# A hybrid decoder block on one core: weight sums of the first four up steps made by accumulating transfers

## The chip, the core and the metric

The kernel runs on one core of a Trainium2 chip. Its time is the device time of one execution in microseconds (us), and a kernel is compared by the median of its runs. The engines of the core are TensorE (PE; PEld is its weight load), VectorE (DVE), ScalarE (ACT), GpSimd (POOL) and SyncE (SP, which here only issues transfers).

## What is computed

One decoder block, in float32, for 1024 tokens of width 1024: attention heads and a chunked gating side by side, their output projection, and then a gated MLP with a causal convolution of three taps, with a norm ahead of each part. Cut to what matters here:

```python
D_MODEL = 1024; SEQ = 1024; D_FF = 2816; CONV_WIDTH = 3

def conv_ffn(x, w_up, conv_w, conv_b, w_down):
    h = x @ w_up                                   # [1024, 1024] @ [1024, 5632]
    h = depthwise_causal_conv(h, conv_w) + conv_b  # 3 taps along the tokens
    a, g = jnp.split(h, 2, axis=-1)
    return (jax.nn.silu(g) * a) @ w_down

    mix = jnp.concatenate([att, sg], axis=-1)      # attention, chunked gating
    h = h + mix @ w_out[layer]
    h = h + conv_ffn(rmsnorm(h, norm_ffn_g[layer]), w_up[layer], ...)
    return rmsnorm(h, norm_final_g)
```

The change concerns `x @ w_up`.

## The kernel before

**Numbers and products.** Every float32 operand of a matmul is split into two parts of a shorter format: ScalarE copies the value to the high part (L153) and VectorE subtracts that from the value to get the low part (L159), both in `split_w`. A product then takes three matmuls: high by high, high by low, low by high.

**The up projection by seven products.** It is made in 22 steps (`NFF`), each for 128 columns of `a` and 128 of `g`. A step takes a weight block of four parts, A11, A12, A21 and A22, and multiplies by the scheme of Strassen and Winograd: seven products instead of eight, three of which take a part as it is (A11, A12, A22) and four of which take a sum of parts:

S1 = A21 + A22, S2 = S1 + A11, S3 = A21 + A11, S4 = S2 + A12.

Each part of a step is a tile of 128 x 512 (256 KB). On the other side stand the activations (XB): B11, B21, B22 and T1 to T4, which are sums of token blocks. In `product` (L999) one product is twelve matmuls. The line is that of all products of the up stage; the names of their outputs tell them apart: `qa` for A11 and A12, `qb` (in step 0 `qc`) for S2, `qc` for S3 and A22, `qd` for S1 and S4.

**Loads and sums of a step.** `upw_a(i)` (L861) loads A11 and A12 as one tile of the ring `raw` (four buffers of 128 x 2 x 512) and later splits them into the ring `wha` (four buffers). `upw_b(i)` (L877) loads A21 and A22 into another `raw` tile and has GpSimd make the four sums (L881 to L889): three or four of them into the ring `sg` (four buffers of 128 x 512), and in step 1 three of them in the place of parts that are no longer needed. `split` of `upw_b` splits A22 and the sums into the ring `whb` (six buffers). In the memory of a step the blocks 0, 1, 2 and 3 of `wup` are A21, A22, A11 and A12.

**Order.** Each engine has its own queue and does its instructions in order. The order of an engine's queue is set by a scheduler from the source order, buffers and dependences, with a few edges added by hand (`behind`, `gates`), so that it isn't that of the source. The order of the products on TensorE is set by hand; the loads and sums of a step are set in motion by a generator, `nxt_of(i)`, which does the preparation of step i + 1 in pieces between the products of step i. The first two steps (`AHEAD = 2`) are prepared earlier: their loads and sums are issued before the tokens' loop below, and their products with A11 and A12 are made ahead of the others and kept in PSUM (`waited`).

**The tokens' loop, ahead of the up steps.** From about 405 to 460 us the output projection is finished for eight tiles of 128 tokens (order 0, 4, 1, 5, 2, 3, 6, 7): matmuls, the residual (`hadd`), the norm (`norm2`), and `flip`, which transposes a tile and makes the activation sums: for the tiles 4 to 7, T2 = B22 + B11 goes into `t2`, a tile with one buffer (VectorE, L958), and GpSimd subtracts from it (L961) to get `xtB21`, the unsplit T4. After the last flip come the splits of S2, S3 and S1 of step 0, those of T1, T4 and B22 (L1023, in two halves each), and then the steps.

**A step** (`up_b(i)`): the products S2, S3, S1, A22 and S4, with the subtractions u2 (L1061), u3 (L1065) and the others on VectorE between them, the convolutions `cg` and `ca` (the last multiplication of a step is L1087), and A11 and A12 of the next step in between (`up_a`). After the last step the down projection follows (L1189), from about 860 us.

Of the kernel before, what the change touches and what calls it, by code (L numbers as in the profile page):

```python
# [12 lines left out]
ALU = mybir.AluOpType  # L13
# [51 lines left out]
def block_kernel(ctx: ExitStack, tc: tile.TileContext, xT, xtok, wuv, wv, wqk, wf, cpk, bfv,  # L65
                 ggain, g2r, gfr, wsp, woa, wos, wup, wdn, out):
    nc = tc.nc
    act, dve, pool, pe, sp = Line(nc.scalar, tc), Line(nc.vector, tc), Line(nc.gpsimd, tc), nc.tensor, nc.sync
# [22 lines left out]
    def sb(tag, shape, dt=F32):  # L91
        return (raws if tag == "raw" else late if tag in LATE else early).tile(shape, dt, tag=tag, bufs=BUFS[tag], name=nm(tag))
# [57 lines left out]
    def split_w(src, hl, hi_eng="act", lo_eng="dve"):  # L150
        h, l = hl
        if hi_eng == "act":
            act.copy(h, src)  # L153
        elif hi_eng == "pool":
            pool.tensor_copy(h, src)
        else:
            dve.tensor_copy(h, src)
        eng = dve if lo_eng == "dve" else pool
        return eng.tensor_tensor(out=l, in0=src, in1=f32(h), op=ALU.subtract)  # L159
# [3 lines left out]
    def behind(inst, key):  # L163

        if key in gates:
            after(tc, inst, gates[key])
# [30 lines left out]
    def ring(dt=F32R):  # L197
        rn[0] += 1
        return sb(RTAG[(rn[0] - 1) % 6], [P, 2, 512], dt)
# [32 lines left out]
    for p_ in range(2):  # L232
        t = sb("G", [P, 2, 2, 512])
# [199 lines left out]
    W = [Weights(0)]  # L433
# [177 lines left out]
    for k in range(4):  # L611
        t = sb("raw", [P, 2, 512])
# [29 lines left out]
    for p_ in range(2):  # L642
        t = ring(F32)
# [207 lines left out]
    def ut_(pool_, tag, shape, dt, bufs):  # L851
        return pool_.tile(shape, dt, tag=tag, bufs=bufs, name=nm(tag))
# [3 lines left out]
    AHEAD = 2  # L856
# [13 lines left out]

        return out, split

    def upw_b(i, out, inplace=False):

        a11, a12 = out["ra"][:, 0, :], out["ra"][:, 1, :]
        wr = sb("raw", [P, 2, 512])
        sp.dma_start(out=wr, in_=wup[i, :, 0:2, :])  # L877
        a21, a22 = wr[:, 0, :], wr[:, 1, :]
        if inplace:
            s = [a21, ut_(upl, "sg", [P, 512], F32, 4), a11, a12]  # L880
            pool.tensor_tensor(out=a11, in0=a21, in1=a11, op=ALU.add)  # L881
            pool.tensor_tensor(out=s[1], in0=a11, in1=a22, op=ALU.add)
            pool.tensor_tensor(out=a21, in0=a21, in1=a22, op=ALU.add)
        else:
            s = [ut_(upl, "sg", [P, 512], F32, 4) for _ in range(4)]
            pool.tensor_tensor(out=s[0], in0=a21, in1=a22, op=ALU.add)  # L886
            pool.tensor_tensor(out=s[1], in0=s[0], in1=a11, op=ALU.add)  # L887
            pool.tensor_tensor(out=s[2], in0=a21, in1=a11, op=ALU.add)
        pool.tensor_tensor(out=s[3], in0=s[1], in1=a12, op=ALU.add)  # L889
        src = {"A22": a22, "S1": s[0], "S2": s[1], "S3": s[2], "S4": s[3]}  # L890

        def split(names):
            for n in names:
                t = ut_(upr, "whb", [P, 2, 512], F32R, 6)
                behind(split_w(src[n], (t[:, 0], t[:, 1])), "sums")
                out[n] = t
            return out

        return split
# [36 lines left out]
    def flip(tt):  # L936

        c = slice((tt % 4) * P, (tt % 4) * P + P)
        pp = []
        for kh in range(2):  # L940
            ps = sbank()
            for j in range(4):
                k = 4 * kh + j
                pe.transpose(ps[:, j * P:(j + 1) * P], xn[tt][:, k * P:(k + 1) * P], ident)
            pp.append(ps.rearrange("p (k t) -> p k t", k=4))
        if tt < 4:
            for n, p3 in (("B11", pp[0]), ("B21", pp[1])):
                hl_of(n, c, p3)
            for n, p3 in (("B11", pp[0]), ("B21", pp[1])):
                act.copy(xt[n][:, :, c], p3)  # L950
            return
        b11, b21, b22 = (xt[n][:, :, c] for n in ("B11", "B21", "B22"))
        t3 = ut_(xtp, "t3", [P, 4, P], F32, 1)
        t2 = ut_(xtp, "t2", [P, 4, P], F32, 1)
        act.copy(b22, pp[1])
        dve.tensor_tensor(out=b11, in0=b11, in1=pp[0], op=ALU.subtract)
        dve.tensor_tensor(out=t3, in0=b22, in1=pp[0], op=ALU.subtract)
        d = dve.tensor_tensor(out=t2, in0=b22, in1=b11, op=ALU.add)  # L958
        hl_of("T2", c, t2)
        hl_of("T3", c, t3)  # L960
        pool.tensor_tensor(out=b21, in0=t2, in1=b21, op=ALU.subtract)  # L961
        return d

    WA = [upw_a(i) for i in range(AHEAD)]
    W = [WA[0][1](("A11", "A12"))]
    first = (0, 4, 1, 5)
    banks8 = {(tt, hf): (bank() if hf == 0 else sbank()) for tt in first for hf in range(2)}
    for tt in first:
        for hf in range(2):
            wmm(tt, hf, banks8[tt, hf], (0, 1, 2))  # L970
    W.append(WA[1][1](("A11", "A12")))
    WB = [upw_b(0, W[0]), upw_b(1, W[1], True)]
    prev = None
    for tt in (0, 4, 1, 5, 2, 3, 6, 7):
        hload(tt)
# [32 lines left out]
    for i in range(AHEAD):  # L1008
# [4 lines left out]
        if i == 0:  # L1013

            last = flip(7)
            WB[0](("S2", "S3"))
            gates["sums"] = last

    def late_sum(n, src):
        for j in range(2):  # L1020
            k = slice(2 * j, 2 * j + 2)
            act.copy(XB[n][:, 0, k, :], xt[src][:, k, :])
            dve.tensor_tensor(out=XB[n][:, 1, k, :], in0=xt[src][:, k, :], in1=f32(XB[n][:, 0, k, :]), op=ALU.subtract)  # L1023

    late_sum("T1", "B11")
    WB[0](("S1",))
    late_sum("T4", "B21")
# [81 lines left out]
    def waited(i):  # L1109

        x1 = ut_(pst_[0], "u", [P, 512], F32, 5)
        ha = ut_(pst_[0], "h", [P, 1024], F32, 3)
        act.copy(x1, ahead[2 * i])
        dve.tensor_tensor(out=ha[:, 0:512], in0=ahead[2 * i + 1], in1=x1, op=ALU.add)
        return None, x1, ha

    st = waited(0)
    WB[0](("A22", "S4"))

    def nxt_of(i):  # L1120

        if i + 1 == NFF:
            while True:
                yield None
        if i + 1 < AHEAD:
            w, wb = W[i + 1], WB[i + 1]
            wa = lambda names: None
        else:
            w, wa = upw_a(i + 1)
            wb = upw_b(i + 1, w)  # L1130
            W.append(w)
        yield None
        wa(("A11",))
        wb(("S2",))
        yield waited(i + 1) if i + 1 < AHEAD else up_a(i + 1, w)
        wa(("A12",))
        wb(("S3",))
        yield None
        wb(("S1", "A22", "S4"))
        yield None  # L1140
# [21 lines left out]
    for p_, n in ((upl, "B11"), (upl, "T2"), (upl, "B21"), (upl, "T3"), (upr, "T1"), (upr, "T4"), (upr, "B22")):  # L1162
        t = ut_(p_, "x" + n, [P, 2, 4, 512], F32, 1)
# [37 lines left out]
    def blk(b):  # L1201
        return lambda p_: wd[p_][:, b, :]
# [129 lines left out]
```

## Time and profile before

| | |
|---|---|
| median of three runs | 1097.8 us (1097.66 to 1100.26) |
| the profiled execution: own time | 1102.1 us |
| the profiled execution: span of its instructions | 1100.4 us |
| mean granted TensorE clock, of full speed | 0.992 |
| bytes read and written in HBM | 114.95 MB and 42.27 MB, 143 GB/s over the span |

The profile is that of one execution. Its busy times are of each engine's instructions by themselves; a row of a group tells the line, the engine, what is written and read, how many there are, their busy time and mean, and then the engine's idle time just before them with what ended most of it. A row of the timeline has the start and the duration of one instruction or of a run of like ones, and in brackets the idle time before it. A row of the table by stretches has the length of the stretch and then the busy time of TensorE, of its weight load, of VectorE, ScalarE and GpSimd, each with the number of instructions in brackets, then the granted clock, the busy share of the 16 transfer engines and the GB/s that they moved. In a row of transfers stand the size of one and the median time from issue to landing. GpSimd issues no transfer of its own in this kernel: the queue of SP carries nearly all of them.

### The profile page before, as it was taken

The page shows a single profiled execution, that of the slowest core. Times are in us where ns is not written, and L with a number is a line of the kernel's source. Part 1 is how long each engine was busy: PE and PEld are TensorE (multiplying, and loading weights), DVE is VectorE, ACT ScalarE, POOL GpSimd, SP SyncE. Part 2 cuts the span into 40 slices and gives each one's busy share as a digit, 9 for nine tenths or more (in the row PEclk, how much of TensorE's full clock was granted, in tenths as well). Part 3 has the DMA queues.
Part 4 walks back from the last instruction along what each step waited for, and adds up shares of the span by engine and source line. Part 5 has one row for each costly group of instructions (what it writes and reads, how often), then busy time and mean ns, then how long its engine had stood idle before and what let it go on. Part 6 is the DMA issues. An engine that isn't in the chain of part 4 may idle for free.

```text
span 1100.4 us, 14437 instructions
## 1 busy us (share of the span) xinstructions
PE 1070.2 (97%) x5013; PEld 880.7 (80%) x5013; DVE 897.8 (82%) x1355; ACT 572.2 (52%) x991; POOL 248.6 (23%) x205
## 2 busy tenths in 40 slices
PE   9999999999998999998999999999999999999997
PEld 6888787777877888776888888888888888888886
DVE  5985799775678859999898989999998875898774
ACT  5666544454467856653444444444444454454653
POOL 0002243133144341334232423333232000000000
PEclk9999999999998999999999999999999999999999
DMA  9242366836576345223133232313321898433342
GB/s 329 96 137 94 97 171 181 254 121 215 189 221 171 97 133 185 86 67 134 68 105 134 85 107 96 126 67 125 115 96 46 268 336 301 140 96 103 125 135 97
DMA packets 64713, 158.18 MB, mean 144 GB/s; under 512 B 7672, under 2 KB 7936, under 8 KB 64640
## 3 DMA queue, kind: packets, MB, share of 16 engines
q1 hardware_dynamic: 64352, 156.70, 43.7%
q8 instruction: 39, 0.64, 0.2%
q10 hardware_dynamic: 288, 0.56, 0.1%
q14 instruction: 34, 0.28, 0.1%
HBM read 114.95 MB, written 42.27 MB: 143 GB/s over the span
## 4 chain that ended last, share of the span: by engine, by line
PE 69%; DVE 7%; ACT 3%; issue 2%; DMA 2%; POOL 1%; SPq 0%; ACTq 0%; POOLq 0%; DVEq 0%
PE k L1189 18%; PE qa L999 10%; PE qd L999 10%; PE qc L999 10%; PE qb L999 5%; PE pb L759 3%; PE ps L256 2%; PE pb L749 2%; PE pf L803 1%; PE pf L804 1%; PE pf L802 1%; DMA x<-ncd 1%; PE ps L730 1%; PE ps L729 1%; DVE whb L159 1%
## 5 line engine op out<-in xcount | busy, mean ns | idle before, releaser
L1189 PE MATMUL k<-whb,wha 128*128 128x512 f32 x924 | 209.7, 389 | 0.0
L1189 PEld LDWEIGHTS k<-whb,wha 128*128 128x128 f32 x924 | 173.5, 188 | 36.1
L999 PE MATMUL qa<-xB,wha 128*128 128x512 f32 x528 | 128.9, 393 | 5.8 <-DVE wha L159 5.8
L999 PE MATMUL qc<-xT,whb 128*128 128x512 f32 x540 | 130.2, 390 | 1.4 <-DVE xT L930 1.4
L999 PEld LDWEIGHTS qa<-xB,wha 128*128 128x128 f32 x528 | 100.0, 190 | 27.4 <-DVE wha L159 6.6
L999 PEld LDWEIGHTS qc<-xT,whb 128*128 128x128 f32 x540 | 101.2, 188 | 23.2 <-DVE xT L930 1.8
L153 ACT CAST wha<-sg 128x512 fp32r<-128x512 f32 x77 | 47.9, 622 | 97.8 <-PE k L1189 87.0
L153 ACT CAST whb<-sg 128x512 fp32r<-128x512 f32 x85 | 51.9, 615 | 69.9 <-PE qc L999 67.7
L159 DVE TENSOR_TENSOR wha<-sg,wha 128x512 fp32r<-128x512 f32 x77 | 53.0, 690 | 40.8 <-ACT wha L153 40.6
L159 DVE TENSOR_TENSOR whb<-sg,whb 128x512 fp32r<-128x512 f32 x85 | 63.0, 743 | 9.1 <-ACT whb L153 8.9
L759 PE MATMUL pb<-pt,V 128*128 128x256 f32 (+1 forms) x320 | 59.4, 303 | 7.0 <-ACT pt L750 4.8
L999 PE MATMUL qd<-xB,whb 128*128 128x512 f32 x264 | 63.8, 389 | 0.1
L999 PE MATMUL qd<-xT,whb 128*128 128x512 f32 x264 | 63.4, 389 | 0.0
L759 PEld LDWEIGHTS pb<-pt,V 128*128 128x128 f32 x320 | 48.3, 194 | 18.6 <-ACT pt L750 11.5
L999 PE MATMUL qb<-xT,whb 128*128 128x512 f32 x252 | 61.0, 389 | 1.0 <-DVE whb L159 1.0
L750 ACT CAST pt<-pb 128x512 fp32r<-128x512 f32 (+1 forms) x80 | 40.8, 545 | 33.4 <-PE pb L749 32.7
L999 PEld LDWEIGHTS qd<-xB,whb 128*128 128x128 f32 x264 | 49.5, 188 | 10.7 <-issue 0.5
L999 PEld LDWEIGHTS qd<-xT,whb 128*128 128x128 f32 x264 | 49.6, 188 | 10.3
L751 DVE TENSOR_TENSOR pt<-pb,pt 128x512 fp32r<-128x512 f32 (+1 forms) x80 | 48.2, 632 | 10.9 <-ACT pt L750 10.2
L887 POOL TENSOR_TENSOR sg<-sg,raw 128x512 f32<-128x512 f32 x21 | 42.5, 2022 | 64.1 <-issue 61.6
L999 PEld LDWEIGHTS qb<-xT,whb 128*128 128x128 f32 x252 | 47.2, 188 | 11.1 <-DVE whb L159 1.4
L886 POOL TENSOR_TENSOR sg<-raw 128x512 f32<-128x512 f32 x21 | 30.6, 1458 | 110.0 <-DVE whb L159 85.6
(378 smaller groups left out, 2308.2 us busy)
## 6 DMA issues: line engine op xcount, KB each, us to landing
raw<-wup SPq DMA_DIRECT2D x44, 512.0 KB, 3.6
sg<-hx SPq DMA_DIRECT2D x77, 256.0 KB, 3.0
hx<-hs SPq DMA_DIRECT2D x44, 256.0 KB, 2.0
hx<-ca SPq DMA_DIRECT2D x33, 256.0 KB, 2.0
xT<-wdn SPq DMA_DIRECT2D x28, 256.0 KB, 4.8
raw<-wqk SPq DMA_DIRECT2D x8, 512.0 KB, 3.6
qd<-G SPq DMA_DIRECT2D x16, 256.0 KB, 4.7
kd<-G SPq DMA_DIRECT2D x16, 256.0 KB, 3.2
```

The lines of the kernel that those rows point to most:

```text
L153: act.copy(h, src)
L159: return eng.tensor_tensor(out=l, in0=src, in1=f32(h), op=ALU.subtract)
L256: pe.matmul(banks[m], xs(n, xi, k)[:, ms], w[:, wi, :], start=(first and k == 0 and c == 0), stop=(k == 3 and c == 2), skip_group_check=True)
L729: pe.matmul(ps[:, 0:e - c], A[:, qs], B[:, c:e], start=True, stop=False)
L749: pe.transpose(ptr[:, c:c + P], tj[jj][:, k * P:(k + 1) * P], ident)
L750: act.copy(pt[:, 0, 0:w], ptr[:, 0:w])
L751: dve.tensor_tensor(out=pt[:, 1, 0:w], in0=ptr[:, 0:w], in1=f32(pt[:, 0, 0:w]), op=ALU.subtract)
L759: pe.matmul(po[:, oo:oo + n], lhs, pt[:, s, o:o + n], start=(k == 0 and s == 0), stop=(s == 1 and half))
L886: pool.tensor_tensor(out=s[0], in0=a21, in1=a22, op=ALU.add)
L887: pool.tensor_tensor(out=s[1], in0=s[0], in1=a11, op=ALU.add)
L999: pe.matmul(ps, w[:, wi, ks], xb[:, xi, k, :], start=(first and n == 0), stop=(n == 11), skip_group_check=True)
L1189: pe.matmul(banks[bk + m], xh[:, xi, ms], wh[:, wi, :], start=(first and p_ == 0 and n == 0), stop=(p_ == NP - 1 and n == 2), skip_group_c ...
```

## The change

In the steps 0 to 3 GpSimd no longer adds. `upw_b(i)` loads A11 once more, into an `sg` tile (plain transfer, SP), and GpSimd issues accumulating transfers, which read a block of `wup` from HBM and add it to what stands in the tile:

- S2 = A11 (the new load) + block 0 + block 1, in the `sg` tile;
- S1 = A21 + block 1, in the place of A21;
- S3 = A11 + block 0, in the place of A11;
- S4 = A12 + blocks 0, 1 and 2, in the place of A12.

Those into the same tile follow one another. S3 and S4 need A11 and A12 split first, since they overwrite them. In the steps 0 and 1 all seven are issued at once; in the steps 2 and 3 those of S3 and S4 are put off (`pend`) until the split of S3 is asked for. From step 4 on the sums are made by GpSimd as before. In all there are 28 accumulating transfers of 256 KB and four more plain loads, and sixteen sums of GpSimd less. The form of step 1 that summed in place goes. Lines from L893 on are 13 further down after the change.

```diff
-    def upw_b(i, out, inplace=False):
+    def upw_b(i, out):
 
         a11, a12 = out["ra"][:, 0, :], out["ra"][:, 1, :]
         wr = sb("raw", [P, 2, 512])
         sp.dma_start(out=wr, in_=wup[i, :, 0:2, :])
         a21, a22 = wr[:, 0, :], wr[:, 1, :]
-        if inplace:
+        blk = lambda b: wup[i, :, b, :]
+        pend = []
+        if i < 4:
+
             s = [a21, ut_(upl, "sg", [P, 512], F32, 4), a11, a12]
-            pool.tensor_tensor(out=a11, in0=a21, in1=a11, op=ALU.add)
-            pool.tensor_tensor(out=s[1], in0=a11, in1=a22, op=ALU.add)
-            pool.tensor_tensor(out=a21, in0=a21, in1=a22, op=ALU.add)
+            sp.dma_start(out=s[1], in_=blk(2))
+
+            def add(*todo):
+                for t, bs_ in todo:
+                    for b in bs_:
+                        pool.dma_start(out=t, in_=blk(b), accum_op=ALU.add)
+
+            add((s[1], (0, 1)), (a21, (1,)))
+            pend.append(lambda: add((a11, (0,)), (a12, (0, 1, 2))))
+            if i < AHEAD:
+                pend.pop()()
         else:
             s = [ut_(upl, "sg", [P, 512], F32, 4) for _ in range(4)]
             pool.tensor_tensor(out=s[0], in0=a21, in1=a22, op=ALU.add)
             pool.tensor_tensor(out=s[1], in0=s[0], in1=a11, op=ALU.add)
             pool.tensor_tensor(out=s[2], in0=a21, in1=a11, op=ALU.add)
-        pool.tensor_tensor(out=s[3], in0=s[1], in1=a12, op=ALU.add)
+            pool.tensor_tensor(out=s[3], in0=s[1], in1=a12, op=ALU.add)
         src = {"A22": a22, "S1": s[0], "S2": s[1], "S3": s[2], "S4": s[3]}
 
         def split(names):
+            if "S3" in names and pend:
+                pend.pop()()
             for n in names:
...
-    WB = [upw_b(0, W[0]), upw_b(1, W[1], True)]
+    WB = [upw_b(0, W[0]), upw_b(1, W[1])]
```

## The prediction

> **What bounds the kernel now.** I read the page first, then the waits of TensorE between 380 and 540 us, then a table of ten-microsecond stretches, then the timelines of VectorE, GpSimd and TensorE around the first four up steps. The page says that TensorE is the bound: busy for 97% of the span, and most of the chain that ended last.
>
> ```profile
> span 1100.4 us, 14437 instructions
> PE 1070.2 (97%) x5013; PEld 880.7 (80%) x5013; DVE 897.8 (82%) x1355; ACT 572.2 (52%) x991; POOL 248.6 (23%) x205
> PE 69%; DVE 7%; ACT 3%; issue 2%; DMA 2%; POOL 1%; SPq 0%; ACTq 0%; POOLq 0%; DVEq 0%
> ```
>
> So an edit to GpSimd's sums pays only where TensorE is idle. The waits of that stretch name the places: the first products of the up steps wait for VectorE. The stretches show the other side: there VectorE (third figure) is busy for 10 of 10 us and TensorE (first) is not, while from 540 us on TensorE has no gap at all.
>
> ```profile
> PE qa L999 <- DVE wha L159: 5.8, 2, 3.9
> PE qc L999 <- DVE xT L930: 1.4, 1, 1.4
> PE qb L999 <- DVE whb L159: 1.0, 1, 1.0
> ...
> 420.00:430.00 10.00, 10.00 (x53) 7.92 (x52) 9.10 (x16) 7.93 (x15) 1.12 (x1) 1.00 0.75 271
> 430.00:440.00 10.00, 10.00 (x54) 8.31 (x53) 10.00 (x16) 6.99 (x14) 1.60 (x1) 1.00 0.54 186
> ...
> 460.00:470.00 10.00, 8.63 (x38) 6.81 (x38) 10.00 (x11) 7.51 (x10) 5.42 (x3) 1.00 0.00 0
> 470.00:480.00 10.00, 9.03 (x40) 6.97 (x39) 10.00 (x14) 3.58 (x7) 2.57 (x2) 1.00 0.16 52
> 490.00:500.00 10.00, 8.03 (x35) 6.00 (x34) 10.00 (x13) 3.47 (x5) 5.34 (x3) 1.00 0.18 59
> 510.00:520.00 10.00, 6.13 (x26) 4.77 (x25) 10.00 (x13) 2.49 (x3) 7.30 (x3) 0.97 0.57 211
> 540.00:560.00 20.00, 20.00 (x90) 16.57 (x89) 18.40 (x21) 8.07 (x13) 6.41 (x4) 1.00 0.29 105
> ```
>
> The waits add to 8.2 us. That is all that steps 0 to 3 can give back.
>
> **What is removed.** Sixteen GpSimd sums go, four for each of steps 0 to 3. None is on the path by itself; what they cost is VectorE's time, because a sum of two SBUF tiles on VectorE stretches while GpSimd runs one:
>
> ```profile
> 461.56 1.72 POOL L889 TENSOR_TENSOR raw<-sg,raw 128x512 f32<-128x512 f32 x1
> 478.72 1.62 POOL L887 TENSOR_TENSOR sg<-sg,raw 128x512 f32<-128x512 f32 x1
> 493.77 1.59 POOL L887 TENSOR_TENSOR sg<-sg,raw 128x512 f32<-128x512 f32 x1 [0.68 <-POOL sg L886]
> ...
> 462.05 2.32 DVE L1023 TENSOR_TENSOR xT<-xtB,xT 128x1024 fp32r<-128x1024 f32 x1
> 466.57 1.21 DVE L1023 TENSOR_TENSOR xT<-xtB,xT 128x1024 fp32r<-128x1024 f32 x1
> 475.25 0.68 DVE L159 TENSOR_TENSOR whb<-sg,whb 128x512 fp32r<-128x512 f32 x1
> 478.25 2.65 DVE L159 TENSOR_TENSOR whb<-raw,whb 128x512 fp32r<-128x512 f32 x2
> 494.76 2.85 DVE L159 TENSOR_TENSOR wha<-raw,wha 128x512 fp32r<-128x512 f32 x2
> ```
>
> The same instruction takes 2.32 beside a GpSimd sum and 1.21 without: 1.1 us. Two splits take 2.65 and 2.85 where two undisturbed ones take about 1.3: 1.35 and 1.55. Together 4.0 us of a VectorE queue that has no gap between the first and the last of them. Up to the A11 product of step 2 TensorE waits 1.4 + 1.0 + 1.9 = 4.3 us (the last is quoted below), so these 4.0 come off the end: **minus 4.0 us**. It can't be more than 4.3, and is nothing if GpSimd's own part in an issue disturbs VectorE as the sums do.
>
> **What is added.** Four plain 256 KB loads (into "sg"; four issues on SP, in a stretch where nothing waits for SP) and 28 accumulating transfers of 256 KB issued by GpSimd. The profile of before has no transfer from GpSimd's queue, so the price of one, from the end of its wait to the landing that the next may wait for (call it A), is bounded by neighbours:
>
> ```profile
> raw<-wup SPq DMA_DIRECT2D x44, 512.0 KB, 3.6
> sg<-hx SPq DMA_DIRECT2D x77, 256.0 KB, 3.0
> hx<-hs SPq DMA_DIRECT2D x44, 256.0 KB, 2.0
> ...
> xT<-wdn SPq DMA_DIRECT2D x28, 256.0 KB, 4.8
> ...
> L886 POOL TENSOR_TENSOR sg<-raw 128x512 f32<-128x512 f32 x21 | 30.6, 1458 | 110.0 <-DVE whb L159 85.6
> L887 POOL TENSOR_TENSOR sg<-sg,raw 128x512 f32<-128x512 f32 x21 | 42.5, 2022 | 64.1 <-issue 61.6
> ```
>
> Below: 2.0, a 256 KB store. Above: 6.0, a read and a write-back of 3.0 each, one after the other. I take 5.0, nearest to the load of the same size and kind: 3.0, plus 0.6 for the second operand (3.6 less 3.0), plus about 1.4, an ordinary GpSimd instruction, as an estimate of GpSimd's own part in an issue. Sums that build on each other cost A each in series, since every one waits for the landing before it: S2 two, S3 and S1 one each, S4 three. A GpSimd sum of before took 1.3 to 2.0.
>
> The Trainium skill (DMA: Bandwidth & Descriptors, section "Anatomy of one DMA — SWDGE (gpsimd) path") gives a GpSimd-issued copy 2.0 us fixed plus bytes over 436 GB/s, so 2.6 for 256 KB. No run here shows it; what it would make of the sum is the first rival.
>
> **Ahead of the loop.** GpSimd's order becomes: 18 accumulations (all of steps 0 and 1, and S2 of steps 2 and 3), then the four subtractions into xtB21 (L961 before, L974 after). Each flip overwrites the one t2 buffer that the subtraction of the flip before still has to read, so VectorE (L958), and all that is queued behind it, waits if GpSimd is late.
>
> ```profile
> 418.07 1.67 POOL L881 TENSOR_TENSOR raw<-raw,raw 128x512 f32<-128x512 f32 x1 [19.57 <-DVE wha L159]
> 432.00 1.60 POOL L961 TENSOR_TENSOR xtB<-t,xtB 128x512 f32<-128x512 f32 x1 [10.88 <-DVE t L958]
> 441.37 0.68 DVE L958 TENSOR_TENSOR t<-xtB,xtB 128x512 f32<-128x512 f32 x1
> ```
>
> The accumulations into places of split blocks can start when L881 could, 418.1. By the order, three rounds of waiting (second and third addition of S4, second of S2 of step 2) and about five issues of 1 us lie ahead of the first subtraction: 418.1 + 5 + 3 x 5.0 = 438.1, and with its 1.6 us 439.7, 1.7 us before VectorE needs it at 441.4. But the transfers share the engines with the loads and stores of the flips. From 271 GB/s at 0.75 busy, all engines move some 360 GB/s, so 256 KB is 0.73 us: 16 of them are 11.7 us of all engines, or 23 if an accumulation moves twice the bytes. Between 418 and 440 the rows leave about 2.5 + 4.6 + 1 = 8 free. So the subtraction is on time if they move once, and up to 8 us late if twice and the flips' transfers go first; VectorE's own slack after it takes some 2. I take **plus 1.5**, range 0 to 6.
>
> **Step 2.** S3 and S4 are now made in the place of A11 and A12, so they start only when VectorE has split those.
>
> ```profile
> 495.97 2.57 PE L999 MATMUL qa<-xB,wha 128*128 128x512 f32 x10 [1.90 <-DVE wha L159]
> 502.68 2.88 PE L999 MATMUL qc<-xT,whb 128*128 128x512 f32 x12
> 510.84 2.88 PE L999 MATMUL qc<-xT,whb 128*128 128x512 f32 x12
> 519.18 4.14 PE L999 MATMUL qa<-xB,wha 128*128 128x512 f32 x10 [3.87 <-DVE wha L159]
> ...
> 508.03 1.22 DVE L1087 TENSOR_TENSOR ca<-ca,cg 128x1024 f32<-128x1024 f32 x1
> ...
> L153 ACT CAST whb<-sg 128x512 fp32r<-128x512 f32 x85 | 51.9, 615 | 69.9 <-PE qc L999 67.7
> ```
>
> In the clock of before, A11 is split at 495.9 (t). S3: t + 5.0 + 0.62 (ScalarE half) + 0.68 (VectorE half) = t + 6.4; its product is due at 502.68 = t + 6.8: just in time. S4: t + 1 + 3 x 5.0 + 1.3 = t + 17.3. Its split now stands in VectorE's order right behind the product that closes step 1's convolution (L1087, done at 509.2 = t + 13.3), and the u3 that the A22 product (510.84, t + 14.9) needs stands behind the split. So VectorE stands still for 4 us with u3 behind it. From the split's end eleven VectorE instructions of 0.6 and about 1.3 us beside GpSimd's sums of step 4 lead to the A11 split of step 3: t + 17.3 + 8.0 = t + 25.3, against t + 23.3 before (519.18). **Plus 2.0.** Break-even at A = 4.3; below 3.7 VectorE's own queue sets it, and 1.4 are gained.
>
> **Step 3.** In GpSimd's order step 4's four ordinary sums stand ahead of step 3's S3 and S4. They need a raw tile that is free only after step 2's S4 was split: t + 17.3 + 0.7, load 3.6, four sums about 6.4 = t + 28.0, which is 2.7 behind step 3's A11 split (t'). S3: t' + 2.7 + 5.0 + 1.3 = t' + 9.0 against t' + 6.8, some 0.3 of it allowed: 1.9 late. S4: t' + 3.7 + 15 + 1.3 and u3's 0.7 = t' + 20.7 against t' + 14.9 + 1.9: 3.9 late. **Plus 5.8.** After that VectorE and TensorE run as before (18.4 of 20 busy): nothing is won back. Step 2's loads now come at about 473 instead of 417, but their splits are needed at 494: hidden, at no cost.
>
> **Sum.** 1.5 - 4.0 + 2.0 + 5.8 = +5.3 us on the profiled execution, 1102.1 us, 4.3 above the median. On the median: 1097.8 + 5.3 = **1103.1 us**. A difference under 0.3%, 3.3 us, can't be told from none here.
>
> **Rivals.**
> Short transfers, the other side. A = 3.3 (2.0 to 3.0, and little of GpSimd's own part): early 0, -4.0, step 2 -1.4, step 3 0.2 + 0.5: -4.7, **1093.1**. It decides below A = 3.6. For it: landings of 2.0 and 3.0; against: three loads of kernel inputs at 3.6 and 4.8, and that an accumulation reads twice. The Trainium skill's 2.6, with the 0.6 added, falls in this case. Chance 0.2.
> Balance. A = 4.1: early 0.5, -4.0, step 2 -0.8, step 3 3.1: -1.2, **1096.6**, no difference. Chance 0.2.
> The engines fill up. An accumulation moves twice the bytes, A = 6.0, early +6, -4.0, step 2 +4.9, step 3 +8.8: +15.7, **1113.5**. For it: 0.75 busy at 420 to 430 already. Against: the stores of h2d there wait for nobody. The Trainium skill (same page, "Issuing engines are not separate DMA queues") says that transfers from GpSimd run on the same 16 engines as SP's; no run here shows it yet. Chance 0.12.
>
> **Chances and range.** The forecast, A of 4.6 to 5.5, plus 3.3 to 11, keeps 0.48. Slower is 0.48 + 0.12 = 0.60, faster 0.20, same 0.20. The range reaches from the short transfers, 1093, to the full engines with two more microseconds of early lateness, 1115; under 2 in 10 lie outside, most of them above.
>
> **What would show it.** Right: in the profile after, the waits of 1.4, 1.0 and 1.9 us before 496 us are gone or half gone; accumulations land 4.6 to 5.5 us after their issue; ScalarE and VectorE wait for a DMA of "raw" from "wup" in steps 2 and 3, and TensorE for xT4's product there and nowhere later. Wrong: landings near 3 us, and TensorE's idle time in 455 to 560 below the 8.2 of before; or a stall of the flips at 441 us larger than all that follows.

## The result, and the profile after

| | before | after |
|---|---|---|
| median | 1099.03 us (1097.66 to 1101.77, 4 runs) | 1123.6 us (1122.0 to 1126.53, 4 runs) |
| the profiled execution, own time | 1102.1 us | 1122.0 us |

The change made the kernel slower by 24.6 us: ratio 1.0221, 95% interval 1.0202 to 1.024. The forecast was 5.3 slower.

First the page of after: span, busy time and the queues (packets, MB, share of 16 engines).

```profile
span 1120.3 us, 14470 instructions
PE 1075.3 (96%) x5013; PEld 882.5 (79%) x5013; DVE 892.4 (80%) x1355; ACT 572.0 (51%) x991; POOL 244.9 (22%) x217
...
q1 hardware_dynamic: 64928, 157.75, 42.4%
q0 software_dynamic: 4032, 7.34, 3.8%
```

Then groups of its transfers (size of one, median us from issue to landing). The last row is that of before, for comparison:

```profile
raw<-wup POOLq DMA_DIRECT2D x20, 256.0 KB, 5.0
...
pt<-hpd SPq DMA_DIRECT2D x8, 512.0 KB, 6.2
...
sg<-wup POOLq DMA_DIRECT2D x8, 256.0 KB, 6.8
...
pt<-hpd SPq DMA_DIRECT2D x8, 512.0 KB, 3.5
```

GpSimd's queue, q0, is new: 3.8% of 1120.3 us is 42.6 us of all engines for 28 transfers, 1.52 us each. SP's q1 takes 42.4%, 475 us for 157.75 MB: 0.79 us for the same 256 KB. An accumulation thus costs the engines 1.9 times a plain transfer. This isn't an effect of the crowding: in e5, e10 and e13 below, where the engines are mostly free, an accumulation takes 1.6 us. The loads of the flips (`pt<-hpd`) land in 6.2 us where it was 3.5. TensorE is busy for 5.1 us longer with as many matmuls: the time isn't all waiting.

The waits of TensorE from 380 to 560 us, and last the one of before on the same tile:

```profile
PE ps L957 <- DVE xn L939: 13.2, 2, 7.9
PE qc L1012 <- ACT whb L153: 4.0, 1, 4.0
PE qc L1012 <- ACT wha L153: 2.1, 1, 2.1
PE qc L1012 <- DVE u L1078: 1.7, 1, 1.7
PE qd L1012 <- DVE h L1084: 1.2, 1, 1.2
PE qb L1012 <- DVE whb L159: 1.0, 1, 1.0
...
PE ps L944 <- DVE xn L926: 0.4, 1, 0.4
```

Stretches of ten microseconds (TensorE, weight load, VectorE, ScalarE, GpSimd, granted clock, share of transfer engines, GB/s):

```profile
420.00:430.00 10.00, 7.03 (x38) 5.32 (x37) 3.66 (x7) 3.86 (x8) 2.38 (x4) 1.00 1.06 290
430.00:440.00 10.00, 7.66 (x27) 6.47 (x28) 9.10 (x16) 6.05 (x12) 3.74 (x5) 0.66 1.05 230
...
450.00:460.00 10.00, 3.12 (x12) 2.87 (x13) 7.46 (x11) 3.52 (x6) 3.42 (x3) 0.57 0.33 74
```

The largest waits stand where before had next to none (0.4 us): in the flips, on the norm (`xn`), 13.2 us in two. The transfer engines are full there (1.06, 1.05), and behind each wait the granted clock is down to 0.66 and 0.57. VectorE's waits from 405 to 475 us say which these are:

```profile
DVE t L971 <- POOL xtB L974: 8.1, 1, 8.1
...
DVE pt L931 <- DMA pt<-hpd: 5.6, 1, 5.6
```

And GpSimd's timeline:

```profile
445.98 0.86 POOL L889 DMA_DIRECT2D sg<-wup  x1 [3.20 <-DMA sg<-wup]
450.09 0.86 POOL L889 DMA_DIRECT2D sg<-wup  x1 [3.25 <-DMA sg<-wup]
450.65 1.60 POOL L974 TENSOR_TENSOR xtB<-t,xtB 128x512 f32<-128x512 f32 x1
```

One is the load of `hpd`, 5.6 us late. The other is the subtraction into xtB21: it stands behind the last accumulation, at 450.65, where before it ran at 432.00; VectorE waits 8.1 us for it with the next flip in hand. GpSimd itself is hardly busy: an issue takes 0.87 us, the rest is waiting.

To see where the time went, I lined up the two traces by TensorE's matmuls, which stand in the same order, and noted by how much each comes later. Executions differ by up to 8 us ahead of the first transfer, so only differences along the way are read, and times in two traces can't be compared as they stand. In us, for all kernels of this study, one execution of each (the stretches in the time of before; the label of each as in the next section; the last column is the difference from the runs of before that were taken with that kernel):

| | flips, 416 to 464 | 464 to 508 | step 2, to 525 | step 3, to 552 | behind, to 606 | sum | median less before's |
|---|---|---|---|---|---|---|---|
| after | +17.9 | -3.6 | -1.4 | +9.5 | +2.4 | +24.7 | +24.6 |
| e1 | +12.8 | -3.5 | -1.2 | +9.7 | +2.2 | +20.0 | +22.2 |
| e2 | +6.2 | -3.5 | -1.8 | +11.8 | +2.4 | +15.1 | +13.3 |
| e4 | +6.5 | +0.1 | -1.6 | 0 | 0 | +5.1 | +6.4 |
| e5 | +0.6 | -2.5 | -0.9 | +9.5 | +2.3 | +8.9 | +9.1 |
| e6 | +5.8 | -3.2 | -4.7 | +5.7 | +2.4 | +6.1 | +5.9 |
| e7 | 0 | -3.5 | -1.2 | 0 | 0 | -4.7 | -5.9 |
| e9 | +4.4 | -3.5 | +0.8 | 0 | +1.1 | +2.7 | +2.1 |
| e10 | 0 | -1.9 | +0.3 | 0 | +1.2 | -0.5 | -1.2 |
| e11 | 0 | -2.5 | -4.3 | +1.6 | +2.4 | -2.7 | -2.9 |
| e12 | 0 | -1.0 | -1.3 | +4.4 | +1.8 | +4.0 | +3.7 |
| e13 | 0 | +1.9 | -2.9 | 0 | 0 | -1.0 | -1.0 |

Two things lose: the flips, 17.9 us, and step 3 with what follows, 11.9. The gain that was sought, 3.6 and 1.4, is there.

### The profile page after: what moved, and what is told of

The parts are those of the page before. It is cut to its first block, busy times and chain, and to the rows that moved or that the text cites. A ratio compares the mean times of both kernels' runs of the same rounds, so it can differ in the third digit from the quotient of the medians.

```text
span 1120.3 us, 14470 instructions
## 1 busy us (share of the span) xinstructions
PE 1075.3 (96%) x5013; PEld 882.5 (79%) x5013; DVE 892.4 (80%) x1355; ACT 572.0 (51%) x991; POOL 244.9 (22%) x217
## 3 DMA queue, kind: packets, MB, share of 16 engines
q1 hardware_dynamic: 64928, 157.75, 42.4%
q0 software_dynamic: 4032, 7.34, 3.8%
## 4 chain that ended last, share of the span: by engine, by line
PE 61%; DVE 7%; issue 6%; DMA 4%; ACT 3%; POOL 2%; SPq 0%; POOLq 0%; ACTq 0%; DVEq 0%
PE k L1202 18%; PE qc L1012 9%; PE qd L1012 8%; PE qa L1012 8%; PE qb L1012 4%; PE pb L759 2%; PE ps L256 2%; DMA raw<-wup 1%; PE pb L749 1%; PE pf L803 1%; PE pf L804 1%; PE pf L802 1%; DMA x<-ncd 1%; PE ps L730 1%; PE ps L729 1%
## 5 line engine op out<-in xcount | busy, mean ns | idle before, releaser
L1012 PE MATMUL qc<-xT,whb 128*128 128x512 f32 x540 | 134.0, 398 | 9.9 <-ACT whb L153 4.0
L159 DVE TENSOR_TENSOR wha<-sg,wha 128x512 fp32r<-128x512 f32 x77 | 52.8, 688 | 42.6 <-ACT wha L153 42.5
L153 ACT CAST whb<-sg 128x512 fp32r<-128x512 f32 x76 | 46.4, 615 | 63.2 <-PE qc L1012 59.4
L159 DVE TENSOR_TENSOR whb<-sg,whb 128x512 fp32r<-128x512 f32 x76 | 56.9, 750 | 8.8 <-ACT whb L153 8.7
L1012 PEld LDWEIGHTS qd<-xB,whb 128*128 128x128 f32 x264 | 49.5, 188 | 11.9 <-issue 1.6
L898 POOL TENSOR_TENSOR sg<-sg,raw 128x512 f32<-128x512 f32 x18 | 37.4, 2078 | 58.2 <-issue 58.0
L1062 DVE SCALAR_TENSOR_TENSOR cg<-h,cp,cg 128x1023 f32<-128x1023 f32 x22 | 37.6, 1711 | 14.9 <-ACT cg L1061 14.9
```

The costliest lines, as they stand in the source:

```text
L1012: pe.matmul(ps, w[:, wi, ks], xb[:, xi, k, :], start=(first and n == 0), stop=(n == 11), skip_group_check=True)
L1062: dve.scalar_tensor_tensor(out=c[:, 1:1024], in0=h[:, 0:1023], scalar=w[1], in1=c[:, 1:1024], op0=ALU.mult, op1=ALU.add)
```

## The experiments

**Is it the order of GpSimd's queue, or the transfers themselves?** In the flips, the landings told by the trace's semaphores show that each accumulation that doesn't wait for its own tile starts 0.25 to 0.31 us after the landing of the third one before it. At most three are in flight, and those issued between 411 and 446 us land 4.4 to 9.9 us later. e1 gives the store for their descriptors half as much again:

```diff
-dynamic_dma_scratch_size=1024
+dynamic_dma_scratch_size=1536
```

> The kernel after, with the store for GpSimd's transfer descriptors 1536 bytes instead of 1024; nothing else. In the trace after, every accumulation between 416 and 442 us that doesn't wait for its own tile starts 0.25 to 0.31 us after the landing of the third one before it. Theory A (the store holds three transfers and so sets the pace of GpSimd's queue): four or five are in flight, the last of the 18 early ones is issued before 447 us instead of at 450.1, the subtraction behind it comes 3 to 5 us earlier, and the kernel takes 1118 to 1121 us against 1123.6. Rival B (the 16 transfer engines are full there, 1.05 busy, and set the pace): more are in flight, each lands later, the last is issued at 449 to 451 as now, 1122 to 1125 us.

Measured: 1123.05 us (ratio 1.0202, 1.0173 to 1.023). Up to five were in flight, so the store does set their number; but each landed later, and the group's median says it:

```profile
sg<-wup POOLq DMA_DIRECT2D x8, 256.0 KB, 9.3
```

9.3 us instead of 6.8. The last early issue was at 450.09 as in after, but in this execution the sixteen transfers that wait for splits began later, at 416.27 instead of 411.93: they were issued within 33.8 us instead of 38.2. VectorE's wait for the subtraction fell from 8.1 to 2.7 us, that for the flips' load rose from 5.6 to 6.5, and the flips lost 12.8 instead of 17.9. The medians don't tell the two kernels apart, so what the store alone costs (theory A said 3 to 6 us) stays open. Five places instead of three made the queue only 4.3 us quicker, and 12.8 us stay: the full engines set the pace more than the store does.

e2 changes the order alone, four transfers to behind the subtractions:

```diff
-                        pool.dma_start(out=t, in_=blk(b), accum_op=ALU.add)
+                        r = pool.dma_start(out=t, in_=blk(b), accum_op=ALU.add)
+                        if i >= AHEAD:
+                            after(tc, r, subs[-1])
```

> The kernel after, with the four accumulations of S2 of steps 2 and 3 put behind the flips' subtractions into xtB21 in GpSimd's order; the other 14 early ones stay ahead of them. Theory A (the order of GpSimd's queue makes VectorE wait 8.1 us at 444 us, and TensorE 7.9 with a lowered clock after it): the subtraction comes at about 436 us, the wait of 8.1 goes, and with the clock some 9 to 10 us are won: 1113 to 1115 us. Rival B (the transfers slow the flips' own loads and stores, whatever the order): at most 3 us are won, 1120 to 1124.

Measured: 1114.11 us (ratio 1.0123, 1.0097 to 1.0149), as theory A has it. GpSimd's timeline of e2:

```profile
437.60 0.86 POOL L891 DMA_DIRECT2D raw<-wup  x1 [1.36 <-DVE pt L935]
438.16 1.62 POOL L978 TENSOR_TENSOR xtB<-t,xtB 128x512 f32<-128x512 f32 x1
```

And VectorE's waits:

```profile
DVE pt L935 <- DMA pt<-hpd: 5.1, 1, 5.1
```

The subtraction runs at 438.16, VectorE's wait of 8.1 is gone, and the flips lose 6.2. What is left is the late load, 5.1. So of 17.9 us, 11.7 came from the four transfers that stood ahead of the subtraction in an in-order queue, and about 6 from the load. (With the order the four also left the stretch of full engines; this run doesn't separate the two.)

**Which steps lose?** e4 accumulates for steps 0 and 1 alone, e5 for steps 2 and 3 alone (with step 1 as before):

```diff
-        if i < 4:
+        if i < AHEAD:           # e4
+        if AHEAD <= i < 4:      # e5
```

> Accumulating transfers for steps 0 and 1 alone; steps 2 and 3 summed by GpSimd as before. Theory A: the flips still lose the first wait (5.3 us of TensorE and 1.8 for the clock), not the second; steps 2 and 3 cost nothing and win nothing but about 1 us from step 1's sum: 6 us over before, about 1105 us. Rival (the loss is that of the 14 transfers and the engines that they fill, not of the four behind them): 12 to 17 us over before, 1111 to 1116. If the steps 2 and 3 were the main loss, within 3 us of before.

> Accumulating transfers for steps 2 and 3 alone; steps 0 and 1 summed by GpSimd as before (step 1 in place). All twelve plus two transfers stand behind the flips' subtractions then. Theory A (flips and steps cost separately): the flips are as before, the splits on VectorE win about 3 us, step 2 loses 4 and step 3 about 7.5 with the lowered clock: 7 to 10 us over before, 1106 to 1109 us. Rival (steps 2 and 3 are late only because the flips made everything late): within 3 us of before, or faster by 3.

Measured: e4 1107.22 us (ratio 1.0065, 1.0045 to 1.0086), e5 1109.93 us (1.0086, 1.0071 to 1.0102). Theory A holds in both: e4 loses in the flips alone, 6.5 us; e5 lies 9.1 us over before, where 7 to 10 were expected, though the loss is all in step 3 and behind; step 2, for which 4 were expected, loses nothing. In e5 the scheduler puts all transfers behind the subtractions, the flips' loads land in 3.2 us, and steps 2 and 3 lose by themselves what they lose in after. The rival, that they are late only because of the flips, falls. TensorE's waits of e5, 420 to 620 us:

```profile
PE qc L1018 <- ACT whb L153: 4.0, 1, 4.0
PE qc L1018 <- DVE u L1084: 3.6, 3, 2.0
PE qc L1018 <- ACT wha L153: 2.5, 1, 2.5
```

**Are the engines full because an accumulation costs twice?** e6 leaves out the adding; the transfers overwrite, so the sums are left out:

```diff
-                        pool.dma_start(out=t, in_=blk(b), accum_op=ALU.add)
+                        pool.dma_start(out=t, in_=blk(b))
```

> The kernel after, with the 28 accumulating transfers made plain ones of the same size and place (they overwrite instead of adding, so the sums are left out). The page of after gives GpSimd's 28 transfers 3.8% of 16 engines' span, 42.6 us or 1.52 us of all engines for each; SP's transfers take 475 us for 157.75 MB, 0.79 us for 256 KB. Theory C (the full transfer engines make the flips' loads late and the landings long): a plain transfer takes half as much, lands in 3 to 5 us, the flips lose 0 to 5 us instead of 17.8, and the chains of three in steps 2 and 3 are a third shorter: 1102 to 1109 us. Rival (GpSimd's in-order queue with three in flight is what is slow, whatever a transfer does): landings of 6 us and more stay between 416 and 450 us, and the kernel takes more than 1115 us.

Measured: 1105.99 us (ratio 1.0056, 1.0033 to 1.0079). Its transfers:

```profile
q0 software_dynamic: 2240, 7.34, 2.0%
...
raw<-wup POOLq DMA_DIRECT2D x20, 256.0 KB, 4.0
```

2.0% of 1105.4 us is 22.1 us, 0.79 for each of the 28: half. The order of GpSimd's queue is that of after, yet VectorE's wait for the subtraction is gone, since the queue is through by 437 us. The flips still lose 5.8 (a wait of 3.6 and a lowered clock), more than theory C's 0 to 5, and landings there were 3.7 to 7.3 us, not 3 to 5. Two things change with the adding: what a transfer takes of the engines, and how many are in flight (up to six plain ones). But with five accumulations in flight e1 still lost 12.8. So the double time on the engines makes the larger part of the loss, and the order makes it felt.

**What is there to win?** e7 leaves the sums of the four steps out altogether.

```diff
-            add((s[1], (0, 1)), (a21, (1,)))
-            pend.append(lambda: add((a11, (0,)), (a12, (0, 1, 2))))
-            if i < AHEAD:
-                pend.pop()()
```

> The kernel after without the accumulating transfers at all: the sums of steps 0 to 3 are left out, the four plain loads stay. It bounds what freeing GpSimd can give. Theory A (all four waits of before, 8.2 us, come from GpSimd's sums on VectorE, and each longer one costs 1.7 us of lowered clock besides): 8 to 11 us under before, 1089 to 1092 us. Rival (two of the four, 1.4 and 1.0, are VectorE's own queue, as the 0.3 and 0.97 that stayed in after say): 5 to 8 us under before, 1092 to 1095.

Measured: 1094.13 us (ratio 0.9947, 0.9927 to 0.9968), 5.9 us under before: the rival's range. TensorE's waits that stay, 420 to 620 us:

```profile
PE qa L1008 <- DVE wha L159: 1.6, 1, 1.6
PE qd L1008 <- DVE h L1080: 1.0, 1, 1.0
PE qb L1008 <- DVE whb L159: 1.0, 1, 1.0
```

Even without any sum VectorE keeps TensorE waiting three times. Some 5 to 6 us is all that this change could win.

**What makes steps 2 and 3 late?** In after, TensorE's timeline:

```profile
517.77 2.88 PE L1012 MATMUL qd<-xT,whb 128*128 128x512 f32 x12
522.76 4.57 PE L1012 MATMUL qc<-xT,whb 128*128 128x512 f32 x12 [2.11 <-ACT wha L153]
...
539.87 4.71 PE L1012 MATMUL qc<-xT,whb 128*128 128x512 f32 x12 [3.98 <-ACT whb L153]
```

VectorE's:

```profile
504.90 1.29 DVE L159 TENSOR_TENSOR wha<-raw,wha 128x512 fp32r<-128x512 f32 x2
...
520.72 0.69 DVE L159 TENSOR_TENSOR whb<-raw,whb 128x512 fp32r<-128x512 f32 x1 [3.08 <-ACT whb L153]
...
527.97 2.66 DVE L159 TENSOR_TENSOR wha<-raw,wha 128x512 fp32r<-128x512 f32 x2
```

GpSimd's:

```profile
527.10 1.28 POOL L897 TENSOR_TENSOR sg<-raw 128x512 f32<-128x512 f32 x1 [10.48 <-DMA raw<-wup]
...
531.73 2.27 POOL L900 TENSOR_TENSOR sg<-sg,raw 128x512 f32<-128x512 f32 x1
533.95 1.77 POOL L889 DMA_DIRECT2D raw<-wup  x2
540.91 0.88 POOL L889 DMA_DIRECT2D raw<-wup  x1 [5.20 <-DMA raw<-wup]
```

Step 2: A11 and A12 are split from 504.90. VectorE stands still for 3.08 us before S4's split at 520.72, and the product that needs u3 behind it waits 2.11. (u3 ended at 522.61. The row names ScalarE, whose casts stood behind the same landing and ended at 522.72.) Step 3: A11 and A12 are split from 527.97, the first by 528.9, but S3's transfer is issued at 533.95, behind step 4's four sums, and its product waits 3.98. And a product takes 4.57 and 4.71 us behind these waits instead of 2.88.

e10 is e5 with S4 made of the finished S2 by one transfer, e12 is e5 with step 4's sums behind step 3's accumulations, e11 has both:

```diff
-            pend.append(lambda: add((a11, (0,)), (a12, (0, 1, 2))))
+            def late():                                       # e10, e11
+                add((a11, (0,)))
+                last3[:] = [pool.dma_start(out=a12, in_=s[1], accum_op=ALU.add)]
+            pend.append(late)
...
-            pool.tensor_tensor(out=s[0], in0=a21, in1=a22, op=ALU.add)
+            r = pool.tensor_tensor(out=s[0], in0=a21, in1=a22, op=ALU.add)
+            if i == 4:                                        # e11, e12
+                after(tc, r, last3[0])
```

> Steps 2 and 3 alone by accumulation, as in the run that was 1109.9 us, and S4 made by one transfer that adds the finished S2 tile to A12 instead of three that add blocks 0, 1 and 2. Theory (the chain of three, 3 x 4 us, makes VectorE stand still with u3 behind it): in step 2 the wait of 2.5 and its 1.7 of clock go; in step 3 S3 stays late behind step 4's sums (4.0 and 1.8), but the 2.0 and 1.3 after it go: 5 to 7 us won, 1103 to 1105 us. Rival (it is the wait for A11 and A12's split and the sums ahead in GpSimd's queue, not the length of the chain): at most 2 us won, 1108 to 1110.

> Steps 2 and 3 alone by accumulation, as in the run that was 1109.9 us, with step 4's four ordinary sums put behind step 3's accumulations in GpSimd's order. Theory A (step 3's S3 is late because the sums of step 4 stand ahead of it): S3 starts when A11 is split, its wait of 4.0 and the 1.8 of clock go, 4 to 6 us won, 1104 to 1106 us. Rival B (the wait moves on: step 4's sums now stand behind a chain of three landings, and its S2 comes late): 1108 to 1114 us.

> Steps 2 and 3 alone by accumulation, S4 by one transfer from the S2 tile, and step 4's ordinary sums behind step 3's accumulations: the two last edits together. The run with the first alone was even with before (ratio 1.000) and kept one wait of 3.1 us for step 3's A11, where VectorE's instructions are stretched by step 4's sums (1.74 for a split of 0.68). Theory (the rest of the loss is this collision and the chain): that wait goes, nothing else comes late, and the kernel is 2 to 4 us under before, 1096 to 1098 us, near the 1094.1 of the run without any sums. Rival (the wait moves to step 4, whose sums now start 5 us later): even with before or up to 3 us over.

Measured: e10 1098.84 us (ratio 1.0, 0.9982 to 1.0019), e12 1103.73 (1.0042, 1.0023 to 1.006), e11 1097.75 (0.9976, 0.9962 to 0.999). The short chain takes back all of the 9.1 us that e5 lay over before, more than was expected, since step 3 comes right with it: the scheduler now puts step 3's two transfers ahead of the last of step 4's sums. GpSimd's timeline of e10:

```profile
520.47 0.88 POOL L891 DMA_DIRECT2D raw<-wup  x1 [2.40 <-DVE wha L159]
521.12 1.12 POOL L896 DMA_DIRECT2D raw<-sg  x1
526.26 1.29 POOL L912 TENSOR_TENSOR sg<-sg,raw 128x512 f32<-128x512 f32 x1 [4.01 <-DMA raw<-sg]
```

S3 starts as soon as A11 and A12 are split (at 519.14, in 1.28 us). e12 shows that the order is a cause by itself: the wait for S3 is gone, step 3 loses 4.4 instead of 9.5, and what is left is S4's chain (a wait of 2.5). e11 takes the remaining wait for step 3's A11 from 3.1 to 1.2 us and has the lowest median of the versions that compute everything, though its interval overlaps that of e13 below. Part of the gain is lost again behind step 3, +2.4; why isn't shown, since after has the same +2.4 with the other order.

e13 keeps S3 and S4 of steps 2 and 3 as GpSimd's sums into fresh tiles:

```diff
-            s = [a21, ut_(upl, "sg", [P, 512], F32, 4), a11, a12]
+            s = [a21] + [ut_(upl, "sg", [P, 512], F32, 4) for _ in range(3)]
...
+            pool.tensor_tensor(out=s[2], in0=a21, in1=a11, op=ALU.add)
+            pool.dma_start(out=a21, in_=blk(1), accum_op=ALU.add)
+            pool.tensor_tensor(out=s[3], in0=s[1], in1=a12, op=ALU.add)
```

> In steps 2 and 3 S2 and S1 by accumulation (three transfers a step, none waiting for a split), S3 and S4 as GpSimd's ordinary sums into fresh tiles; steps 0 and 1 as before. Theory (what wins is fewer sums on GpSimd beside VectorE's splits; what loses is everything that has to wait for a split or a chain): half of the sums remain, so about half of the 4 to 5 us that the run without sums won: 1 to 3 us under before, 1097 to 1099 us. Rival (the transfers ahead of them in GpSimd's queue make S3 and S4 late): 2 to 6 us over before.

Measured: 1099.65 us (ratio 0.9987, 0.9975 to 0.9999), the low end of what was expected. By the table the stretch from 464 to 508 loses 1.9 us here, where the other versions with fewer sums win. e9 is the short chain in all four steps, with e2's order:

```diff
+                r = pool.dma_start(out=a12, in_=s[1], accum_op=ALU.add)
+                if i >= AHEAD:
+                    after(tc, r, subs[-1])
```

> All four steps by accumulation as in the kernel after, with S4 made by one transfer from the S2 tile, and with nothing but steps 0 and 1's ten transfers ahead of the flips' subtractions. Theory (the flips lose by what the transfers take of the engines, 1.5 us each, 14 of them 6.2 to 6.5 us): ten cost 2 to 4 us, the steps behind are those of the run that was even with before: 1102 to 1105 us. Rival (one late load is enough, however few transfers): the flips lose 6 as with 14, 1106 to 1108 us.

Measured: 1102.77 us (ratio 1.0008, 0.9991 to 1.0024), even with before. With ten transfers ahead the flips lose 4.4 us, against 6.2 with 14: fewer is less, though a little more than the 2 to 4 expected.

## Why the prediction was wrong

The direction was right, and the step that failed is the one **ahead of the loop**: +1.5 (0 to 6) was said and 17.9 came. Of the signs that the prediction named for being wrong, the last one came: a stall of the flips larger than all that follows, 17.9 against 6.9. Three parts of this step were wrong.
- The rounds. I counted three rounds of waiting at 5.0 us, as if transfers that don't build on each other all went at once. At most three were in flight, so the 16 issued from 411.9 us on made more than five rounds, to 450.1 us. e1 shows that the number is the store's, and that it alone doesn't make the loss: with five, 12.8 us stay.
- The engines. I had worked out both ends, 11.7 and 23 us of all engines for 16, and that the subtraction would be up to 8 us late at the second; 1.52 us each makes 24.3, and it was late by 8.1 us of VectorE's time. The rival of the full engines had the mechanism right, except that "twice the bytes" is not what the profile counts: 7.34 MB in after and in e6 alike, but 1.8 times the packets and 1.9 times the engines' time. Its +6 left out that the flips' own loads come late as well (5.6 us), which e2 and e4 show by themselves. The Trainium skill (DMA: Bandwidth & Descriptors, section "Issuing engines are not separate DMA queues") says that transfers run on the same 16 engines whichever engine issued them. The trace agrees: `pt<-hpd` from SP's queue went from 3.5 to 6.2 us.
- The clock. Every wait was priced at its length. The two waits add to 13.2 us, against 0.4 before; the rest of 17.9 is the slow clock behind them, where the same matmuls keep TensorE busy for 5.1 us longer.

**The relief of VectorE**, -4.0: -3.6, about right. Of the waits of 1.4 and 1.9, 0.3 and none are left, 3.0 us less; the other 0.6 is busy time of the matmuls. The wait of 1.0, which was counted in, stayed, and e7 shows that it does so even without sums. e7 also shows the bound, some 5 to 6 us.

**The price of one transfer**, 5.0: too low where the engines are full (4.4 to 9.9) and a little high where they are free. The three links of S4's chain in step 2 took 13.45 us, 4.5 each, and e5's two groups have medians of 3.9 and 4.3. That the `raw` group of after has a median of just 5.0 is luck: it mixes both. The Trainium skill's formula (DMA: Bandwidth & Descriptors, section "Anatomy of one DMA — SWDGE (gpsimd) path") gives an estimate of 2.6 us for a copy of this size. No accumulating transfer here met it, and the `raw` group of e6, plain ones, landed in 2.9 us at best and 4.0 at the median: the measurement decides.

**Step 2**, +2.0: -1.4. The mechanism was as described, VectorE idle before S4's split with u3 behind it, 3.08 us instead of 4. But the A11 of step 3 was split by 528.9, 23.3 us after that of step 2 (505.6), as before, and not 25.3. Of these 2.0 us the shorter links of the chain gave 1.5 (S4's split ended 15.8 us after step 2's A11, not 17.3), and VectorE's way from there the other 0.5 (7.5 us, not 8.0). TensorE, held up at u3 by 2.11 and the clock, no longer waited for it, and before's 3.87 with its own slow clock went: the wait moved and got shorter.

**Step 3**, +5.8: +9.5 and 2.4 behind it. The sums of step 4 ended 28.4 us after step 2's A11 (t + 28.0 was said), but with A11 at t + 23.3, S3 came 5.1 us behind it, not 2.7. Its product's wait of 3.98 cost 1.8 more by the clock. S4's lateness cost a wait of 1.7 for u3, where 3.9 was said. That nothing is late behind step 3 was wrong too. (A slip in the sum without effect: t + 5.0 + 0.62 + 0.68 is t + 6.3, not t + 6.4.)

The terms behind the flips, -4.0 + 2.0 + 5.8 = +3.8, came out at +6.9; the flips' 16.4 us make most of the error.

## What to carry to other kernels

Moving sums from an idle-looking engine to its transfer queue turns 1.6 us of work into 4 to 10 us of latency in the same in-order queue: count what else stands in that queue (here one small subtraction), how many transfers it keeps in flight, and what each takes of the shared engines, which for an accumulation was 1.9 times a copy. Let accumulations build on a finished sum instead of repeating its terms, and issue them where the transfer engines are free; so done, for two steps alone, the idea wins 0.2% (0.1 to 0.4). Price a wait of TensorE with the slow clock behind it.

## What the runs showed of the hardware

- An accumulating transfer of 256 KB takes 1.52 us of all sixteen engines (after), a plain one 0.79 us, from either queue (SP's in after, GpSimd's in e6). With 1024 bytes of descriptor store at most three accumulations were in flight (after), with 1536 at most five (e1); of plain ones up to six with 1024 (e6).
- A short wait of TensorE can slow what follows. Twelve matmuls of the up products, from the start of the first to the start of what follows them, take 2.7 us. Over all runs of this study, the dozens of up products right behind a wait were read: of 32 waits of 0.9 to 1.5 us none slowed it, they took 2.8 to 3.0 (one more had a second wait within the dozen); of 7 of 1.57 to 1.96 us four did, to 4.1 to 4.5 us; of 8 from 2.1 to 2.7 us six; and all eight of 2.9 us and more, to 4.2 to 5.3. The granted clock over the slowed dozens was 0.50 to 0.67, over the others 1.00. So a wait above two microseconds mostly costs some 1.5 us more. The Trainium skill (TensorE: Matmul & The Clock Gate, section "HAM oscillation — how this bites in real kernels") has the rule that gaps above about 3.4 us are to be avoided; here half of that sufficed at times.
